# Second MLP products with shifted stationary operands (layer 0) and passes outermost (layer 1); third groups' scores in two column tiles

## The chip, the cores and the metric

The kernel runs on one core of a Trainium2 chip. The metric is the device time of one execution in microseconds (us). Before the change two executions were timed: 2586.64 and 2588.89 us, median 2587.76 us.

The core's engines are named as in the profile: PE is TensorE's matmul stream and PEld its loads of stationary operands, DVE is VectorE, ACT is ScalarE, POOL is GpSimd, and SP issues most of the DMAs.

## The reference

Two decoder layers on `x` of 1 x 1024 x 1024 in float32. Layer 0 mixes tokens with dilated sliding-window attention (8 heads, three groups of window and dilation (128, 1), (512, 4), (2048, 16)), layer 1 with gated linear attention; each is followed by an MLP with a squared ReLU.

```python
def dilated_attention(h, w_in, w_out):
    qkv = (h @ w_in).reshape(B, S, N_GROUPS, 3, ATTN_HEADS, HEAD_DIM)
    for g, (window, dil) in enumerate(DILATED_GROUPS):
        q = apply_rope(qkv[:, :, g, 0], cos, sin) * (HEAD_DIM ** -0.5)
        k = apply_rope(qkv[:, :, g, 1], cos, sin)
        o_g, lse_g = dilated_group_attention(q, k, qkv[:, :, g, 2], dil, window // dil)
    ...
def sq_relu_mlp(h, w_up, w_down):
    a = jax.nn.relu(h @ w_up)
    return (a * a) @ w_down

for i in range(DEPTH):
    h = rmsnorm(x, norm_mix_w[i])
    x = x + (dilated_attention(...) if i % 2 == 0 else gla_mixer(...))
    h = rmsnorm(x, norm_mlp_w[i])
    x = x + sq_relu_mlp(h, mlp_w_up[i], mlp_w_down[i])
return rmsnorm(x, final_norm_w)
```

The two products of an MLP are 1024 x 1024 by 1024 x 4096 and 1024 x 4096 by 4096 x 1024. The change touches the second one in both layers, and the scores q·k of the third attention group.

## The kernel before, in words

**Precision.** Large products are made in three passes. Each float32 operand is split into a rounded part (`h`, hi) and its remainder (`l`, lo), both of type fp32r; the sum is hi·hi + hi·lo + lo·hi, three matmuls into the same accumulator. ACT makes the hi part and DVE the lo part (`split`, lines 219 to 223). Scores and values of the attention are plain float32 matmuls, and the program runs each of those as two rows of the profile.

**Order.** All instructions are written out in the order in which each engine runs them (a manual schedule); semaphores carry only the dependences. PE's order in the attention comes from a clock of steps (`at`, `advance`), in which `Attention.plan` puts the four score blocks of a group at fixed steps, between matmuls of the next group's projection (`Heads.run_head`, which calls `Up.product`, line 599).

**The second MLP product** (`Down`). The product is computed in a scheme with 7 block products instead of 8 (`q` from 0 to 6, with the operand names in `ORDER`). Each has 8 steps `m`, so that there are 56 steps `n`. In step n:

- `product(n)` (line 1947) issues 24 matmuls 128x128 by 128x512: two contraction blocks `k`, four row blocks `t`, three passes. The stationary operand is a 128-column slice of the activations' parts (`sh`, `sl`), the moving one a row of the weights' parts (`th`, `tl`). Each row block `t` has a PSUM bank of its own: four banks `pA` or four banks `pB`, by the parity of q.
- `prep(n + 2)` makes the four parts of the step after next: `dh`, `dl` of the activations `sin`, `dh`, `dl` of the weights `t`.
- `fetch(n + 5)` and `load(n + 5)` issue the DMAs of `sin` and of the weights on SP.

Layer 0 has `spill` set (it writes its residual stream to DRAM), layer 1 has `spill` None.

**Memory.** SBUF tiles come from pools of equal slots. `k4` has 25 slots of 4096 bytes per partition, `h8` has 12 of 8192. A tile waits for the release of the slot that it gets. Every operand of the large matmuls lies in `k4` or `h8`, at a slice that begins at a multiple of 512 bytes, and the two pools' first slots differ by a multiple of 4096 bytes; so the start of a stationary slice and that of the moving slice differ by a multiple of 512 bytes. The exception is `wboth` (line 2418), a small gate weight of layer 1, whose eight stationary slices are 96 columns wide and 384 bytes apart.

**Scores of a group** (`Attention.scores`, line 989). For each head and group there are four calls `j` of two 128-row blocks. `keys_of` gives the keys of a block: one block of 128 keys for the third group (g = 2). There, each of the 8 heads has 8 products of 128x128 by 128x128.

Of the kernel before, what the change touches and what calls it, by code (L numbers as in the profile page):

```python
# [10 lines left out]
F32R = mybir.dt.float32r  # L11
# [9 lines left out]
P = 128  # L21
# [21 lines left out]
def hybrid_trunk(ctx, tc, x, norm_mix, norm_mlp, norm_fin, a_in, a_out, g_in, g_up, g_b, g_nw,  # L43
                 g_out, m_up, m_down, tab, msk, gmask, ident_d, out):
    nc = tc.nc
    pe, act, dve, pool, sp = nc.tensor, nc.scalar, nc.vector, nc.gpsimd, nc.sync

    cst = ctx.enter_context(tc.tile_pool(name="cst", bufs=1))
    wk = ctx.enter_context(tc.tile_pool(name="wk", bufs=1))
# [4 lines left out]
    def h8(shape, dt, name):  # L54
        return wk.tile(shape, dt, name=name, tag="h8", bufs=12)

    def k4(shape, dt, name):
        return wk.tile(shape, dt, name=name, tag="k4", bufs=25)

    def t2(shape, dt, name):  # L60
        return wk.tile(shape, dt, name=name, tag="t2", bufs=8)
# [7 lines left out]
    def bank(name):  # L69
        return psp.tile([P, 512], F32, name=name, tag="ps", bufs=8)  # L70
# [41 lines left out]
    class Weights:  # L112
# [17 lines left out]
        def dma(self):  # L130
            n = self.ndma
            if n < len(self.slots):
                self.ndma += 1
                src = self.slots[n]
                self.raws[n] = k4([P] + list(src.shape[1:]), F32, "raw")
                sp.dma_start(self.raws[n], src)

        def prep(self, eng=dve):
            n = self.nprep
            while self.ndma <= n:  # L140
                self.dma()
            src = self.raws.pop(n)
            self.nprep += 1
            if src.shape[-1] == RANK:
                both = self.both = k4([P, KT, 6 * RANK], F32R, "wboth")
                hi, lo = both[:, :, :RANK], both[:, :, RANK:2 * RANK]
            else:
                hi = k4(list(src.shape), F32R, "whi")
                lo = k4(list(src.shape), F32R, "wlo")
            by = self.by[n]  # L150
            if by is None:
                act.activation(hi, src, AF.Copy)
                eng.tensor_tensor(lo, src, hi.bitcast(F32), op=OP.subtract)
            else:
                act.activation(hi, src, AF.Copy, scale=by)
                eng.scalar_tensor_tensor(lo, src, by, hi.bitcast(F32), op0=OP.mult, op1=OP.subtract)
            if src.shape[-1] == RANK:
                for i in range(1, 3):
                    act.activation(both[:, :, 2 * RANK * i:2 * RANK * i + 2 * RANK], both[:, :, :2 * RANK], AF.Copy)
            self.parts[n] = (hi, lo)  # L160
# [57 lines left out]
    def split(hi, lo, src, on_act=True):  # L218
        if on_act:
            act.activation(hi, src, AF.Copy)  # L220
        else:
            dve.tensor_copy(hi, src)
        dve.tensor_tensor(lo, src, hi.bitcast(F32), op=OP.subtract)  # L223
# [277 lines left out]
    class Up:  # L501
# [82 lines left out]
        def product(self, p, s, ks=range(4)):  # L584
            w = self.part[p]
            if s == 6:
                wh, wl = w["d"][:, 0], w["d"][:, 1]
            else:
                wh, wl = (t[:, s % 2] for t in w["aabbgg"[s]])
            h = self.h[self.OPERANDS[s]]  # L590
            st = self.st.setdefault(p, {})
            b = "XYXVXZV"[s]
            first = s in (0, 1, 3, 5)
            if first and ks[0] == 0:
                st[b] = bank("p" + b)
            for k in ks:
                xh, xl = h.parts(k)
                for n, (u, v) in enumerate(((wh, xh), (wh, xl), (wl, xh))):
                    pe.matmul(st[b], u[:, k, :], v, start=first and k + n == 0, stop=k == 3 and n == 2,  # L599
                              skip_group_check=True)  # L600
# [351 lines left out]
    def keys_of(g, b):  # L952

        if g == 0:
            return (128 * (b - 1), 2, 0) if b else (0, 1, 128)
        if g == 1:
            return (256 * (b // 2), 2, 0) if b % 2 else (128 * b, 1, 128)
        return (128 * b, 1, 256)
# [20 lines left out]
    class Attention:  # L979
# [4 lines left out]
        def scores(self, j):  # L984
            ps = bank("pS").rearrange("p (i k) -> p i k", i=2)
            for i in range(2):
                b = 2 * j + i
                k0, n, m0 = keys_of(self.g, b)
                pe.matmul(ps[:, i, :128 * n], self.qT[:, 128 * b:128 * b + 128], self.kT[:, k0:k0 + 128 * n],
                          start=True, stop=True)  # L990
            self.st[j] = ps
# [771 lines left out]
    for p in range(heads.count):  # L1763
# [3 lines left out]
        if p == heads.count - 1:  # L1767
            for k in range(0, KT, 2):
                add_rows(a_out, k)
            c = 14 * p  # L1770
# [103 lines left out]
    class Down:  # L1874
# [32 lines left out]
        def prep(self, n):  # L1907
            if n >= 56:
                return
            q, m = divmod(n, 8)  # L1910
            kept = lambda x: x[m // 2][:, 2 * (m % 2):2 * (m % 2) + 2, :]
            sub = lambda o, a, b: dve.tensor_tensor(o, a, b, op=OP.subtract)  # L1912
            if q in (0, 4):
                t = self.raw.pop(n)
            elif q == 1:
                t = kept(self.br)
            elif q == 2:
                t = kept(self.tc)
                sub(t, t, kept(self.br))
            elif q == 3:  # L1920
                t = kept(self.tc)
                sub(t, self.raw.pop(n), t)
            elif q == 5:
                t = kept(self.br)
                sub(t, kept(self.tc), t)
            else:
                t = self.raw.pop(n)
                sub(t, t, kept(self.tc))
            got = []
            for src in (self.sin.pop(n), t):  # L1930
                hi, lo = k4([P, 2, 512], F32R, "dh"), k4([P, 2, 512], F32R, "dl")
                split(hi, lo, src)
                got += [hi, lo]
            self.cut[n] = got

        def product(self, n, blocks=range(4)):
            q, m = divmod(n, 8)
            s = "BABABAB"[q]
            fresh = q in (0, 1, 2, 6)
            if fresh and m == 0:  # L1940
                self.acc[s] = [bank("p" + s) for _ in range(4)]
            sh, sl, th, tl = self.cut[n]
            for k in range(2):
                for t in blocks:
                    c = slice(128 * t, 128 * t + 128)
                    for v, (a, b) in enumerate(((sh, th), (sh, tl), (sl, th))):
                        pe.matmul(self.acc[s][t], a[:, k, c], b[:, k, :], start=fresh and m + k + v == 0,  # L1947
                                  stop=m == 7 and k == 1 and v == 2, skip_group_check=True)

        def add(self, s, half, t, n):  # L1950
            tb = 4 * half + t
# [460 lines left out]
    for half in range(2):  # L2412
        ps = bank("pd")
# [70 lines left out]
```

## Time and profile before

| | |
|---|---|
| executions timed | 2586.64 and 2588.89 us, median 2587.76 |
| profiled execution, span from the first to the last instruction | 2586.6 us |
| PE busy | 2571.7 us (99%), 12000 matmul rows |
| PEld busy | 2142.3 us (83%) |
| DVE, ACT, POOL busy | 1862.7 (72%), 1298.2 (50%), 45.6 us (2%) |
| DMA | 443.73 MB, mean 172 GB/s |

The profiled execution's own time is not listed apart from its span; the two timed executions lie 0.0 and 2.3 us above that span. A line of the profile's fifth part or of its groups reads: line, engine, operation, out<-in by the program's names, shape, count, then the busy time of the group in us and the mean duration of one in ns. In a name `out<-in,in` the moving operand comes first, so `pB<-dl,dh` has the weights' remainder moving over the activations' rounded part. Matmuls overlap: each row lasts until its last result is out, while the next one has already begun. The rate is therefore read from the starts, or from the busy time of a group divided by its count, not from the mean duration.

The layers' second MLP products lie at 1257 to 1600 us (layer 0) and 2274 to 2587 us (layer 1); the attention's heads at about 265 to 880 us.

### The profile page before, as it was taken

The numbers are of one execution on the slowest core, as the hardware profiler recorded it, in microseconds if no ns is written. First come the engines' busy times: TensorE is split into PE (matmuls) and PEld (weight loads), VectorE is DVE, ScalarE is ACT, GpSimd is POOL, SyncE is SP. The second block draws the span as 40 slices with busy tenths as digits, with TensorE's granted clock in tenths as the row PEclk, the third lists the DMA queues.
The fourth block names the chain that finished last, engine by engine and source line by source line (L and its number), as shares of the span: only waits on it lengthen the run. The fifth ranks groups of instructions, "written<-read, shape, count | busy, mean of one in ns | idle before, by whom it ended". The sixth has DMA issues, their size and how long they took to land.

```text
span 2586.6 us, 33218 instructions
## 1 busy us (share of the span) xinstructions
PE 2571.7 (99%) x12000; PEld 2142.3 (83%) x12000; DVE 1862.7 (72%) x3018; ACT 1298.2 (50%) x2359; POOL 45.6 (2%) x71
## 2 busy tenths in 40 slices
PE   9999999999999999999999999999999999999998
PEld 7888888888888888888888888888888888888887
DVE  7745888888888768666566578887658766666567
ACT  7422455656665456555533345654326555553334
POOL 0000000000000000000000000000000000000000
PEclk9999999999999999999999999999999999999999
DMA  5543577778887634544865353463613544495544
GB/s 183 171 139 118 147 184 202 190 198 199 193 206 189 213 114 159 174 140 155 297 232 193 133 186 102 136 191 98 216 59 107 173 160 149 135 359 198 185 148 131
DMA packets 377544, 443.73 MB, mean 172 GB/s; under 512 B 64178, under 2 KB 240178, under 8 KB 377379
## 3 DMA queue, kind: packets, MB, share of 16 engines
q1 hardware_dynamic: 373650, 430.79, 54.1%
q0 software_dynamic: 3584, 10.56, 1.3%
q8 instruction: 94, 1.54, 0.2%
q14 instruction: 72, 0.58, 0.1%
q10 hardware_dynamic: 144, 0.26, 0.0%
HBM read 279.19 MB, written 126.62 MB: 157 GB/s over the span
## 4 chain that ended last, share of the span: by engine, by line
PE 64%; DVE 2%; ACT 1%; issue 0%; SPq 0%; DMA 0%; ACTq 0%; DVEq 0%
PE pB L1947 13%; PE pX L599 10%; PE pA L1947 10%; PE pV L599 7%; PE pY L599 3%; PE pZ L599 3%; PE pd L216 3%; PE pd L214 3%; PE pd L215 3%; PE pB L830 3%; PE pA L830 2%; PE pT L335 1%; PE pO L2245 1%; PE pU L2227 0%; PE pO L2244 0%; PE pT L260 0%
## 5 line engine op out<-in xcount | busy, mean ns | idle before, releaser
L1947 PE MATMUL pB<-dh 128*128 128x512 f32 x512 | 199.4, 389 | 0.0
L1947 PE MATMUL pB<-dh,dl 128*128 128x512 f32 x512 | 199.2, 389 | 0.0
L1947 PE MATMUL pB<-dl,dh 128*128 128x512 f32 x512 | 199.2, 389 | 0.0
L223 DVE TENSOR_TENSOR dl<-sin,dh 128x1024 fp32r<-128x1024 f32 x112 | 136.5, 1219 | 43.8 <-ACT dh L220 43.1
L220 ACT ACTIVATE dh<-sin 128x1024 fp32r<-128x1024 f32 x112 | 117.9, 1052 | 89.4 <-PE pB L1947 33.2
L220 ACT ACTIVATE dh<-kept 128x1024 fp32r<-128x1024 f32 x64 | 67.9, 1061 | 182.6 <-DVE kept L1912 137.8
L599 PE MATMUL pV<-s4h,wd 128*128 128x512 f32 x448 | 150.8, 398 | 0.0
L1947 PE MATMUL pA<-dh 128*128 128x512 f32 x384 | 149.4, 389 | 0.0
L1947 PE MATMUL pA<-dl,dh 128*128 128x512 f32 x384 | 149.4, 389 | 0.0
L1947 PE MATMUL pA<-dh,dl 128*128 128x512 f32 x384 | 149.4, 389 | 0.0
L1005 ACT ACTIVATE pt<-pt,orow 128x128 f32<-128x128 f32 (+1 forms) x192 | 84.5, 442 | 67.2 <-DVE orow L1003 65.4
L1947 PEld LDWEIGHTS pB<-dh,dl 128*128 128x128 f32 x512 | 96.1, 188 | 20.1
L1947 PEld LDWEIGHTS pB<-dl,dh 128*128 128x128 f32 x512 | 96.1, 188 | 19.8
L1947 PEld LDWEIGHTS pB<-dh 128*128 128x128 f32 x512 | 96.1, 188 | 19.8
L537 DVE TENSOR_TENSOR wal<-raw,wah 128x512 fp32r<-128x512 f32 x112 | 76.1, 685 | 41.4 <-ACT wah L536 41.4
L537 DVE TENSOR_TENSOR wbl<-t,wbh 128x1024 fp32r<-128x1024 f32 x56 | 68.6, 1225 | 44.0 <-ACT wbh L536 43.9
L608 ACT ACTIVATE c<-c 128x512 f32<-128x512 f32 x64 | 40.4, 631 | 118.5 <-DVE c L636 77.5
L599 PEld LDWEIGHTS pV<-s4h,wd 128*128 128x128 f32 x448 | 84.2, 188 | 17.7 <-DVE rb L624 0.2
L223 DVE TENSOR_TENSOR dl<-kept,dh 128x1024 fp32r<-128x1024 f32 x64 | 78.3, 1224 | 24.4 <-ACT dh L220 18.4
L599 PE MATMUL pZ<-a22h,wgh 128*128 128x512 f32 x224 | 89.9, 401 | 0.0
L604 ACT ACTIVATE e<-pX 128x512 f32<-128x512 f32 x96 | 56.5, 588 | 65.2 <-PE pX L599 65.0
L599 PE MATMUL pX<-s3h,wgh 128*128 128x512 f32 x224 | 88.6, 395 | 0.2 <-ACT e L1166 0.2
(398 smaller groups left out, 7397.5 us busy)
## 6 DMA issues: line engine op xcount, KB each, us to landing
sin<-acts SPq DMA_DIRECT2D x112, 512.0 KB, 3.8
raw<-in_mlp_w_up_dram SPq DMA_DIRECT2D x64, 512.0 KB, 5.7
acts<-s SPq DMA_DIRECT2D x64, 512.0 KB, 3.4
raw<-in_mlp_w_down_dram SPq DMA_DIRECT2D x64, 512.0 KB, 4.7
raw<-in_attn_w_in_dram SPq DMA_DIRECT2D x98, 256.0 KB, 4.9
cw<-c SPq DMA_DIRECT2D x192, 128.0 KB, 2.8
acts<-c SPq DMA_DIRECT2D x64, 256.0 KB, 2.2
kept<-in_mlp_w_down_dram SPq DMA_DIRECT2D x32, 512.0 KB, 4.7
```

What stands on the lines that cost most here:

```text
L214: pe.matmul(ps, sh, mh, start=start, stop=False)
L215: pe.matmul(ps, sh, ml, start=False, stop=False)
L216: pe.matmul(ps, sl, mh, start=False, stop=stop)
L220: act.activation(hi, src, AF.Copy)
L223: dve.tensor_tensor(lo, src, hi.bitcast(F32), op=OP.subtract)
L537: self.remain(lambda: dve.tensor_tensor(lo, src, hi.bitcast(F32), op=OP.subtract))
L599: pe.matmul(st[b], u[:, k, :], v, start=first and k + n == 0, stop=k == 3 and n == 2, skip_group_check=True)
L604: act.activation(e, self.st[p]["X"], AF.Copy)
L608: act.activation(r, r, AF.Relu)
L830: pe.matmul(self.acc[s][t], a[:, c], b[:, k, :], start=fresh and m + k + v == 0, stop=m == 1 and k == 1 and v == 2, skip_group_check=True)
L1005: act.activation(pt[:, i, :128 * n], pt[:, i, :128 * n], AF.Exp, scale=-1.0, bias=m, accum_out=self.row[:, r, HD:HD + 1])
L1947: pe.matmul(self.acc[s][t], a[:, k, c], b[:, k, :], start=fresh and m + k + v == 0, stop=m == 7 and k == 1 and v == 2, skip_group_check=True)
```

## The change

- Slots of `k4` become 1056 float32 wide (4224 bytes, 8 x 512 + 128) and there are 24 of them, not 25. A tile can begin at an offset `by` inside its slot.
- In layer 0's second MLP product the activations' parts (the stationary operands) begin at `4 * q + 4` float32 in their slots, 16 bytes for q = 0 up to 112 bytes for q = 6. The moving operands, and both operands of layer 1, begin at 0.
- In layer 1's second MLP product, for q = 0, 2 and 4, the three passes become the outer loop and the four row blocks the inner one. The other q keep their order.
- The third group's score products are issued as two matmuls of 64 stationary columns each, which write rows 0 to 63 and 64 to 127 of the same PSUM region.

What is computed is the same, with the same number of fp32r matmuls. All engines but PE keep the same instructions in the same order; the waits for `k4` slots differ, since tiles now fall into other slots.

```diff
-    def k4(shape, dt, name):
-        return wk.tile(shape, dt, name=name, tag="k4", bufs=25)
+    def k4(shape, dt, name, by=0):
+        t = wk.tile([P, 1056], dt, name=name, tag="k4", bufs=24)
+        n = math.prod(shape[1:])
+        t = t[:, by:by + n]
+        if len(shape) == 3:
+            return t.rearrange("p (a b) -> p a b", b=shape[2])
+        if len(shape) == 4:
+            return t.rearrange("p (a b c) -> p a b c", b=shape[2], c=shape[3])
+        return t
...
                 k0, n, m0 = keys_of(self.g, b)
+                if self.g == 2:
+                    for c in (0, 64):
+                        pe.matmul(ps[c:c + 64, i, :128], self.qT[:, 128 * b + c:128 * b + c + 64], self.kT[:, k0:k0 + 128],
+                                  start=True, stop=True)
+                    continue
                 pe.matmul(ps[:, i, :128 * n], self.qT[:, 128 * b:128 * b + 128], self.kT[:, k0:k0 + 128 * n],
...
             for src in (self.sin.pop(n), t):
-                hi, lo = k4([P, 2, 512], F32R, "dh"), k4([P, 2, 512], F32R, "dl")
+                by = 0 if src is t or self.spill is None else 4 * q + 4
+                hi, lo = k4([P, 2, 512], F32R, "dh", by), k4([P, 2, 512], F32R, "dl", by)
                 split(hi, lo, src)
...
             sh, sl, th, tl = self.cut[n]
+            both = ((sh, th), (sh, tl), (sl, th))
             for k in range(2):
-                for t in blocks:
+                order = [(t, v) for t in blocks for v in range(3)]
+                if self.spill is None and q in (0, 2, 4):
+                    order = [(t, v) for v in range(3) for t in blocks]
+                for t, v in order:
+                    a, b = both[v]
                     c = slice(128 * t, 128 * t + 128)
-                    for v, (a, b) in enumerate(((sh, th), (sh, tl), (sl, th))):
-                        pe.matmul(self.acc[s][t], a[:, k, c], b[:, k, :], start=fresh and m + k + v == 0,
-                                  stop=m == 7 and k == 1 and v == 2, skip_group_check=True)
+                    pe.matmul(self.acc[s][t], a[:, k, c], b[:, k, :], start=fresh and m + k + v == 0,
+                              stop=m == 7 and k == 1 and v == 2, skip_group_check=True)
```

Two places on PE show what moves. The first is in layer 0's attention, the first head's third group: the first two of its four calls, between matmuls of the next projection (`pX`, `pV`). Before:

```order
L599 MATMUL pX_2540<-s2h_617,wbl_2481 128x512
L989 MATMUL pS_2662<-kT_2558,qT_2437 128x128 x2
L989 MATMUL pS_2665<-kT_2558,qT_2437 128x128 x2
L599 MATMUL pV_2623<-s4h_695,wd_2562 128x512
L599 MATMUL pV_2623<-s4l_696,wd_2562 128x512
```

and after:

```order
L606 MATMUL pX_2540<-s2h_617,wbl_2481 128x512
L998 MATMUL pS_2662<-kT_2558,qT_2437 64x128 x4
L998 MATMUL pS_2667<-kT_2558,qT_2437 64x128 x4
L606 MATMUL pV_2623<-s4h_695,wd_2562 128x512
L606 MATMUL pV_2623<-s4l_696,wd_2562 128x512
```

Nothing else moves there: four products of 128 rows have become eight of 64 rows, at the same place in PE's order. The second place is one contraction block of the first product (q = 0) of layer 1's second MLP product; the number of a `pB` is its row block's PSUM bank. Before:

```order
L1947 MATMUL pB_19205<-dh_19133,dh_19129 128x512
L1947 MATMUL pB_19205<-dl_19134,dh_19129 128x512
L1947 MATMUL pB_19205<-dh_19133,dl_19130 128x512
L1947 MATMUL pB_19206<-dh_19133,dh_19129 128x512
L1947 MATMUL pB_19206<-dl_19134,dh_19129 128x512
L1947 MATMUL pB_19206<-dh_19133,dl_19130 128x512
```

and after:

```order
L1964 MATMUL pB_19269<-dh_19197,dh_19193 128x512
L1964 MATMUL pB_19270<-dh_19197,dh_19193 128x512
L1964 MATMUL pB_19271<-dh_19197,dh_19193 128x512
L1964 MATMUL pB_19272<-dh_19197,dh_19193 128x512
L1964 MATMUL pB_19269<-dl_19198,dh_19193 128x512
L1964 MATMUL pB_19270<-dl_19198,dh_19193 128x512
```

Before, three matmuls in a row went to one bank and the stationary part changed after two of them; after, four in a row have the same moving operand, each goes to another bank, and the stationary slice changes at each.

## The prediction

> **What bounds the kernel now.** I read the page first, then PE's waits, then the rate of PE in the stages that the change touches. From the page, the busy times, the granted clock and the head of the chain that ended last:
>
> ```profile
> span 2586.6 us, 33218 instructions
> PE 2571.7 (99%) x12000; PEld 2142.3 (83%) x12000; DVE 1862.7 (72%) x3018; ACT 1298.2 (50%) x2359; POOL 45.6 (2%) x71
> ...
> PEclk9999999999999999999999999999999999999999
> ...
> PE 64%; DVE 2%; ACT 1%; issue 0%; SPq 0%; DMA 0%; ACTq 0%; DVEq 0%
> ```
>
> PE is busy in 2571.7 of 2586.6 us, and the clock is granted in full throughout (a 9 is 90% or more). PE's own waits, longest first:
>
> ```profile
> PE pS L989 <- DVE qT L1146: 1.6, 4, 0.6
> PE warm L1373 <- POOL warm L1348: 1.3, 1, 1.3
> PE pO L1069 <- ACT pt L1018: 0.9, 1, 0.9
> PE pB L830 <- DVE dl L815: 0.8, 1, 0.8
> ```
>
> The longest sum is 1.6 us, so no wait is worth removing and the time is PE's: the number of matmuls times what each takes. A busy PE is not PE at its peak, so the rate per matmul matters. For line 1947, the second MLP product, over the whole span and over 280 us of layer 1 in which nothing else runs on PE (columns: stretch, its length, PE busy with count, PEld busy with count):
>
> ```profile
> 0.00:2587.00 2587.00, 610.16 (x2688) 504.43 (x2688) 1.00 0.56 172
> 2280.00:2560.00 280.00, 280.00 (x1237) 231.86 (x1236) 1.00 0.61 206
> ```
>
> 610.16 us / 2688 is 227.0 ns for each; in the undisturbed stretch 1236 intervals fill 280 us, 226.5 ns. The starts show that it is the same in every pass (layer 0):
>
> ```profile
> 1399.66 0.39 PE L1947 MATMUL pA<-dl,dh 128*128 128x512 f32 x1
> 1399.89 0.39 PE L1947 MATMUL pA<-dh,dl 128*128 128x512 f32 x1
> 1400.12 0.39 PE L1947 MATMUL pA<-dh 128*128 128x512 f32 x1
> 1400.34 0.39 PE L1947 MATMUL pA<-dl,dh 128*128 128x512 f32 x1
> ```
>
> The first interval keeps the stationary operand's part and changes the moving one's, the second and the third change the stationary slice, the third also the PSUM bank between row blocks; all are 0.22 to 0.23 us.
>
> **The change part by part.**
>
> *Passes outermost, layer 1.* The same 24 matmuls and 24 loads of a step come in another order; there are 3 x 8 x 24 = 576 of them. Every kind of neighbour that the new order has (same moving operand with another bank, a change of the stationary slice at each) occurs in the rows above at the same interval, and each matmul has its own load already (x2688 against x2688), so none is saved. Cost 0. The lo part of the moving operand is needed three matmuls later at a step's start, which PE did not wait for anyway.
>
> *Distances, layer 0.* 7 x 8 x 24 = 1344 matmuls get stationary slices 16 to 112 bytes away from the old alignment. Can alignment matter? The one fp32r product whose stationary slices do not lie at multiples of 512 bytes from the moving ones is `wboth`, 96 columns wide and 384 bytes apart. Its row and the first row of the next half frame eight matmuls:
>
> ```profile
> 1722.55 0.39 PE L2418 MATMUL pd<-a11h,wboth 128*96 128x512 f32 x1
> ...
> 1723.25 0.39 PE L2418 MATMUL pd<-a11l,wboth 128*96 128x512 f32 x1
> 1723.48 0.40 PE L2418 MATMUL pd<-a11h,wboth 128*96 128x512 f32 x1
> ...
> 1724.40 0.39 PE L2418 MATMUL pd<-a12h,wboth 128*96 128x512 f32 x1
> ```
>
> 1.85 us / 8 is 231 ns, 4.5 above the 226.5 of the other products although less is loaded. So the interval is not a constant of the form; whether the distance or the width does it, these rows cannot tell. The lower bound is the fastest 512-wide interval in the trace, that of the bfloat16 warming matmuls:
>
> ```profile
> 7.40 0.38 PE L1373 MATMUL warm<-warm 128*128 128x512 bf16 x1
> 7.40 1.46 PE L1373 MATMUL warm<-warm 128*128 128x512 bf16 x6
> ```
>
> (1.46 - 0.38) / 5 = 0.216 us, 11 ns less than 227. The term lies between 1344 x -11 ns = -14.8 us and 1344 x +4.5 ns = +6.0 us. I take 0, by the 2688 rows of the same form, which no slot pair changes. The Trainium skill, "TensorE: Matmul & The Clock Gate", Part 2, says that TensorE reads its moving operand and its loads through two independent ports, so that loading the next operand takes nothing from the running matmul; by that the term is 0 at any distance, and the `wboth` rows are what the trace has against it.
>
> *Slots of 4224 bytes.* 4224 is 8 x 512 + 128, so all operands in `k4`, in every large product, now differ by multiples of 128 bytes and no longer of 512. I take 0 for this by the same row; it is the third rival.
>
> *One slot of `k4` fewer.* Loads are already held back by slots; from SP's waits, the two largest at line 1888, and from the tile `sin`, the time its DMAs take:
>
> ```profile
> SPq L1888 <- PE pB L1947: 144.3, 31, 9.9
> SPq L1888 <- PE pA L1947: 134.8, 30, 7.0
> DMA to landing us min/median/max: 3.4/3.8/13.8
> ```
>
> On SP all later loads and stores are queued behind such a wait. A step is 24 x 0.227 = 5.4 us and takes about six `k4` tiles, so a slot comes on average 0.9 us later and at worst one step. A load is issued five steps ahead and used by `prep` three steps later, 16.3 us; less the 3.8 us to land that leaves 12.5, more than 5.4. The preparation runs two steps (10.9 us) ahead; its pieces:
>
> ```profile
> L220 ACT ACTIVATE dh<-sin x112: 1040/1047/1081, 1247.5 to 2556.5; 128x1024 fp32r<-128x1024 f32 x112
> L223 DVE TENSOR_TENSOR dl<-sin,dh x112: 1210/1218/1228, 1248.6 to 2559.4; 128x1024 fp32r<-128x1024 f32 x112
> L1912 DVE TENSOR_TENSOR kept<-kept x32: 1211/1217/1220, 1318.7 to 2513.3; 128x1024 f32<-128x1024 f32 x32
> ```
>
> Done one after the other without overlap, two of the first, two of the second and one of the third are 5.7 us, against the 5.4 that a delay of a whole step would leave: 0.3 us late where the worst comes together, and cover everywhere else. Between 0 and, with such a miss at every seventh of the 107 steps, 15 x 0.3 = 4.6 us; I take 2. A gain is excluded, since fewer slots release nothing earlier.
>
> *Scores in two column tiles.* 8 heads x 8 products are 64, run as two rows each: 128 of the 208 rows of this group are the third group's. The timeline at the first head's third group:
>
> ```profile
> L989 PE MATMUL pS<-kT,qT 128*128 128x128 f32 x208 | 32.6, 275 | 1.7 <-DVE qT L1146 1.2 <-DVE c L1129 0.6
> ...
> 328.46 0.39 PE L599 MATMUL pX<-s2h,wbl 128*128 128x512 f32 x1
> 328.69 1.05 PE L989 MATMUL pS<-kT,qT 128*128 128x128 f32 x8
> 329.49 0.48 PE L599 MATMUL pV<-s4h,wd 128*128 128x512 f32 x1
> 329.81 0.40 PE L599 MATMUL pV<-s4l,wd 128*128 128x512 f32 x1
> ```
>
> From 328.69 to 329.81 there are eight score rows and one 512-wide matmul: (1.12 - 0.227) / 8 = 0.112 us for a row; the change of form costs nothing beside it. All 128 rows are 14.3 us of PE. After the change they are 256 rows with half the stationary columns but the same 128 moving ones.
> Side by side, two halves take what one whole took, and only the last row of a sequence stands alone. There are 18 sequences (two per head, and four for the last head, whose calls stand apart): 18 x 0.112 = +2.0 us. One after the other: 128 more rows, +14.3 us. Below: if a half row cost a quarter of a whole one, 256 x 0.028 = 7.2, a gain of 7.2 us, for which no row speaks.
> To this comes what PE pays on entering and leaving the divided form, 36 times. No row shows it. If PE must finish the running matmul first, it is that matmul's tail, 0.389 (the mean of a 512-wide row) less 0.227 = 0.162 us, 5.8 us in all; at the other end 0, as at the change from 512-wide to score rows above. If the next load also cannot run ahead, 0.19 us more each time (59.2 us for 384 loads overlap; one lasts 190 ns), 6.8 us:
>
> ```profile
> L989 PEld LDWEIGHTS pS<-kT,qT 128*128 128x128 f32 x384 | 59.2, 190 | 10.9 <-DVE qT L1146 2.5 <-DVE c L1129 1.0 <-PE pO L1069 0.7
> ```
>
> I take side by side with the tail, 2.0 + 5.8 = +7.8 us; the ends are -7.2 and 14.3 + 5.8 + 6.8 = +26.9 us. The Trainium skill, "TensorEngine Tiling (Array Packing)", Key Properties, says that tiles load and multiply in parallel and that a change of the tiling mode drains TensorE; the trace has no divided matmul to confirm either. Without a drain the sum would be 5.8 us less.
>
> *Sum.* 2586.6 + 0 + 0 + 2 + 7.8 = 2596.4 us against the profiled span. The median of the timed runs lies 1.2 us above that span, which gives 2597.6, or 2597.
>
> **The rivals.**
>
> 1. *The halves run one after the other*, in the 18 places of layer 0's attention. For it: PE's matmuls begin in order, and the rows of one product are strictly spaced by 0.112 us. Against it: nothing in the trace. +14.3 + 5.8 + 2 gives 2587.8 + 22 = 2610 us, 2617 with loads that cannot run ahead. This is the slower end; it decides as soon as a half row takes more than half of 0.112 us.
> 2. *The distances free layer 0's matmuls.* At 216 ns in all seven passes -14.8 us, 2583; at some of them in between. If the slot pitch alone did this for line 1947 and for the 1094.57 us of line 599 too, (2688 + 4704) x -11 ns = -81 us, 2516.
>
> ```profile
> 0.00:2587.00 2587.00, 1094.57 (x4704) 877.78 (x4704) 1.00 0.56 172
> ```
>
> 3. *The new pitch spoils the regular interval.* If operands at 128-byte multiples run as the `wboth` rows do, three slot pairs of four are hit: 7392 x 3/4 x 4.5 ns = +25 us, 2623; more if the bad intervals are the rule. It would pass +2% (42 us more than the forecast) from 7.6 ns for each of those 5544 matmuls.
> 4. *The lost slot starves PE* at every step, 0.3 us x 107 = 32 us in place of 2, 2628. The 12.5 us of slack of the loads speaks against it.
> 5. *Nothing shows*: no drain, side by side, no distance effect. +2 to +4 us; it lies beside the forecast and shares its chance.
>
> **How the numbers follow.** Forecast with the fifth case 0.46, first rival 0.22, second 0.14, third 0.14, fourth 0.04. The likeliest gives 2597 us. The range reaches down to 2575 (all seven distances free and the scores at no cost, 2587.8 - 14.8 + 2) and up to 2624 (the first rival's 2617 and the third's 2623); left out are what is worse in the third and fourth and a pitch that frees the whole kernel. One measurement of this kernel can tell about 2%, 52 us, from no change: below 2536 only the second rival in its widest form comes (0.02), above 2639 the third at its worst or the fourth with the first (0.04), within 2% the rest (0.94).
>
> **What would show it.** Right: line 1964's group at 227 ns for a matmul in both layers and in all q; 256 score rows at line 998 whose starts interleave, with the next `pV` about 1.2 us after the first row of a sequence; PE's sums of waits still of a few us. Wrong: intervals that differ between the stretches of the seven q, or in line 606; 16 score rows that take 1.8 us; SP's wait at line 1900 turning into PE waits for `dh` or `dl`.

## The result, and the profile after

The kernel after the change takes 2630.88 us (2630.61 and 2631.15 us), before it 2587.76 us: ratio 1.0167, 95% interval 1.0137 to 1.0196, 43.1 us more. The prediction said 2597 us with a range up to 2624 us; the time lies above that range. From the page of the changed kernel, span and PE's busy time:

```profile
span 2629.4 us, 33543 instructions
...
PE 2616.3 (100%) x12128; PEld 2143.3 (82%) x12128; DVE 1867.2 (71%) x3018; ACT 1299.4 (49%) x2359; POOL 45.6 (2%) x71
```

PE was busy in 2571.7 us and is now in 2616.3 us, 44.6 more; the whole loss is longer PE work. The longest of PE's waits:

```profile
PE warm L1385 <- POOL warm L1360: 1.3, 1, 1.3
...
```

No wait is longer than before (the longest sum was 1.6 us), so the missing slot does not make PE wait. Which matmuls became longer is seen in the busy time by line. First line 606 (the product that was line 599), then line 1964 (the second MLP product, line 1947 in the kernel before), over the whole span; then line 1964 in layer 0 and in layer 1:

```profile
0.00:2630.00 2630.00, 1112.40 (x4704) 879.25 (x4704) 1.00 0.54 169
0.00:2630.00 2630.00, 623.84 (x2688) 504.92 (x2688) 1.00 0.54 169
...
1277.94:1593.80 315.86, 312.85 (x1344) 252.25 (x1343) 1.00 0.58 198
2311.34:2622.40 311.06, 310.99 (x1344) 252.29 (x1343) 1.00 0.56 194
```

Line 1964 rose from 610.16 to 623.84 us, 232.1 ns for each in place of 227.0. It did so in both layers: 232.8 ns in layer 0, where operands are shifted, but 231.4 ns also in layer 1, where none is. Line 606, which the change doesn't name at all, rose from 1094.57 to 1112.40 us. What these have in common is the pool `k4`. The starts in layer 0 (q = 3), the first and the last of eleven rows:

```profile
1421.77 0.39 PE L1964 MATMUL pA<-dl,dh 128*128 128x512 f32 x1
...
1424.08 0.40 PE L1964 MATMUL pA<-dh,dl 128*128 128x512 f32 x1
```

The ten intervals between the eleven starts take 2.31 us, 231 ns each; in the rows of before in the prediction they were 0.22 or 0.23 us. The third groups' scores, at the same place as in the prediction:

```profile
332.84 0.39 PE L606 MATMUL pX<-s2h,wbl 128*128 128x512 f32 x1
333.16 1.09 PE L998 MATMUL pS<-kT,qT 128*64 128x128 f32 x16
334.19 0.50 PE L606 MATMUL pV<-s4h,wd 128*128 128x512 f32 x1
334.52 0.39 PE L606 MATMUL pV<-s4l,wd 128*128 128x512 f32 x1
```

From the last matmul ahead of the scores to the second one behind them it is 1.68 us; before it was 329.81 - 328.46 = 1.35 us. A sequence of four products costs 0.33 us more. The trace has 17 sequences (the prediction counted 18, but two of the last head's calls stand together), so 5.6 us is the estimate for all.

### The profile page after: what moved, and what is told of

It is laid out like the page before. It is cut to its first block, busy times and chain, and to the rows that moved or that the text cites. A ratio compares the mean times of both kernels' runs of the same rounds, so it can differ in the third digit from the quotient of the medians.

```text
span 2629.4 us, 33543 instructions
## 1 busy us (share of the span) xinstructions
PE 2616.3 (100%) x12128; PEld 2143.3 (82%) x12128; DVE 1867.2 (71%) x3018; ACT 1299.4 (49%) x2359; POOL 45.6 (2%) x71
## 4 chain that ended last, share of the span: by engine, by line
PE 97%; DVE 1%; DMA 1%; ACT 1%; issue 0%; SPq 0%; ACTq 0%; DVEq 0%
PE pX L606 17%; PE pB L1964 13%; PE pV L606 12%; PE pA L1964 10%; PE pB L837 8%; PE pA L837 6%; PE pZ L606 6%; PE pY L606 6%; PE pd L221 3%; PE pd L223 3%; PE pd L222 3%; PE pO L1081 2%; PE pS L1001 2%; PE pT L342 1%; PE pB L1481 1%; PE pS L998 1%
## 5 line engine op out<-in xcount | busy, mean ns | idle before, releaser
L1964 PE MATMUL pB<-dh 128*128 128x512 f32 x512 | 178.6, 394 | 0.0
L1964 PE MATMUL pB<-dl,dh 128*128 128x512 f32 x512 | 178.2, 394 | 0.0
L1964 PE MATMUL pB<-dh,dl 128*128 128x512 f32 x512 | 178.1, 393 | 0.0
L606 PE MATMUL pX<-s2h,wbh 128*128 128x512 f32 x224 | 89.0, 397 | 0.0
```

## The experiments

The theory to be tested: the pitch of 4,224 B (the distance from one slot to the next) is the cause, because operand starts now differ by changing multiples of 128 B in every fp32r product that uses `k4`. Rivals: the seven distances of layer 0, the missing slot, the order of the passes.

**One part alone: the pitch.** The kernel before with the 24 new slots, and nothing else.

```diff
-        return wk.tile(shape, dt, name=name, tag="k4", bufs=25)
+        t = wk.tile([P, 1056], dt, name=name, tag="k4", bufs=24)
+        n = math.prod(shape[1:])
+        t = t[:, :n]
...
```

> The kernel before with one thing of the change: the 24 slots of 4,224 B instead of 25 of 4,096 B (every tile still begins at its slot's first byte; layer-0 distances, pass order and whole scores as before). Theory (the pitch makes operand starts differ by changing multiples of 128 B in every fp32r product that takes an operand from these slots, so that the interval no longer holds at 226.7 ns): +37 to +41 us, ratio 1.014 to 1.016, with intervals of 231 to 232 ns in both layers, and no row of waits over 2 us. Rival (the seven distances of layer 0 are what costs): within +-5 us. Rival (the lost slot costs): +37 to +41 us as well, but with new waits of PE in the list of waits and intervals of 226.7 ns between them.

Measured: 2623.58 us against 2587.24 us, ratio 1.0141 (1.0126 to 1.0156), +36.3 us, a little under the 37 to 41 us expected. The page, and the busy time of lines 606 and 1954 (first and second MLP products here):

```profile
span 2621.3 us, 33269 instructions
...
PE 2609.2 (100%) x12000; PEld 2145.5 (82%) x12000; DVE 1866.0 (71%) x3018; ACT 1298.5 (50%) x2359; POOL 45.6 (2%) x71
```

```profile
0.00:2630.00 2630.00, 1112.15 (x4704) 879.38 (x4704) 1.00 0.54 169
0.00:2630.00 2630.00, 622.49 (x2688) 505.10 (x2688) 1.00 0.54 169
```

Five sixths of the loss come with the new slots. The two lines rose by 17.6 and 12.3 us, 3.7 and 4.6 ns for each matmul. PE's busy time rose by 37.5 us in all, while the rest of the span, 14.9 us before, shrank to 12.1: together the 34.7 us between the two spans.

**All but the pitch and the distances.** The kernel after with 24 slots of 4,096 B and all tiles at their slots' first bytes: the missing slot, the passes outermost and the half scores stay.

```diff
-        t = wk.tile([P, 1056], dt, name=name, tag="k4", bufs=24)
+        t = wk.tile([P, 1024], dt, name=name, tag="k4", bufs=24)
...
-                by = 0 if src is t or self.spill is None else 4 * q + 4
+                by = 0
```

> The kernel after with slots of 4,096 B (24 of them) and without the distances of layer 0: what remains is the slot that is missing, the passes outermost in layer 1 and the scores in halves. Theory (pitch): +4 us over before (2 to 7), the scores in halves alone (27.3 us in the after trace against 23.4 before), intervals back at 226 to 227 ns. Rival (lost slot or passes outermost cost): +35 us or more, as after. Rival (layer-0 distances): +4 to +20 us.

Measured: 2592.11 against 2587.24 us, ratio 1.0019 (1.0010 to 1.0029), +4.9 us. Line 1964:

```profile
0.00:2630.00 2630.00, 610.16 (x2688) 504.52 (x2688) 1.00 0.54 169
```

Line 1964 takes 610.16 us, to the last digit what it took before, although 576 of its matmuls come with the passes outermost. So the pass order costs nothing and frees nothing. The +4.9 us lie within the 2 to 7 us expected.

**The disputed cost by itself.** A probe issues 72 matmuls per series, in the order of a step, and varies only where the operands begin (`SH`, `SL`, `TH`, `TL` are multiples of 512 B; `hi`, `lo`, `tl` the shifts in float32):

```diff
+        both = ((SH + hi, TH), (SH + hi, TL + tl), (SL + lo, TH))
+        for r in range(reps):
+            for k in range(2):
+                order = [(t, v) for t in range(4) for v in range(3)]
...
+                for t, v in order:
+                    a, b = both[v]
+                    mm(ps, a + 512 * k + step * t, b + 512 * k, n)
```

> A probe, not the kernel: it leaves out the whole reference computation (its output is a copy of x and one PSUM bank) and issues only the matmuls in question, so only the profile's intervals count. Each series is 72 matmuls (128 stationary columns by 512 moving columns, fp32r) in the order of a step of the second MLP product: first part by first part, first part by remainder, second part by first part. The series differ in where the stationary parts and the moving remainder begin past a multiple of 512 B from the moving first part. The interval of a series is its busy time less 162 ns, over 72. Theory (operand starts): one constant distance in a series may be regular whatever it is, near 226.7 ns as in the second MLP products of before; series with distances that change from matmul to matmul (names with two or three y) stand 4 to 6 ns higher, as in the trace after (229.6 to 232.4 ns). Rival (a distance is good or bad by itself): series of one distance already differ by 4 ns or more. Rival (nothing in TensorE depends on operand starts): all series within 1 ns of each other. The same probe has passes outermost (theory and prediction: no difference), narrower stationary operands, and float32 128x128 products whole and as two 64-column halves: 2 to 16 products, halves cheaper by some 109 ns against 0.2 us per whole product, with an entry and exit of some 0.1 to 0.5 us for each sequence.

The groups by tile, in the view's order of busy time. `dNNNNx` has both stationary parts NNNN bytes from the moving ones, `m000y128y000x` the second part alone at 128 B, `outer0x` the passes outermost, `w96x` 96 columns at multiples of 512 B and `w96by384x` at multiples of 384 B:

```profile
L35 PE MATMUL d0096x<-big 128*128 128x512 f32 x72 | 17.0, 396 | 0.0
...
L35 PE MATMUL d0128x<-big 128*128 128x512 f32 x72 | 17.0, 395 | 0.0
...
L35 PE MATMUL d0384x<-big 128*128 128x512 f32 x72 | 17.0, 395 | 0.0
...
L35 PE MATMUL w96by384x<-big 128*96 128x512 f32 x72 | 16.9, 394 | 0.0
...
L35 PE MATMUL m000y128y000x<-big 128*128 128x512 f32 x72 | 16.8, 394 | 0.0
...
L35 PE MATMUL w96x<-big 128*96 128x512 f32 x72 | 16.7, 392 | 0.0
...
L35 PE MATMUL d0192x<-big 128*128 128x512 f32 x72 | 16.6, 391 | 0.0
...
L35 PE MATMUL outer0x<-big 128*128 128x512 f32 x72 | 16.5, 389 | 0.0
...
L35 PE MATMUL d0016x<-big 128*128 128x512 f32 x72 | 16.5, 389 | 0.0
L35 PE MATMUL d0256x<-big 128*128 128x512 f32 x72 | 16.5, 389 | 0.0
L35 PE MATMUL d0000x<-big 128*128 128x512 f32 x72 | 16.5, 389 | 0.0
```

A group's busy time is 71 intervals and the last row's own duration. The same for `d0000x` and `d0128x`, in this order, from the windows, which have two decimals:

```profile
0.00:1446.50 1446.50, 16.48 (x72) 13.51 (x72) 1.00 0.02 7
...
0.00:1446.50 1446.50, 16.96 (x72) 13.51 (x72) 1.00 0.02 7
```

(16.48 - 0.389) / 71 = 226.6 ns at 0 B, (16.96 - 0.395) / 71 = 233.3 ns at 128 B. My expectation that one constant distance would be regular whatever it is fell: series of one constant distance already differ. In this probe 0, 16 and 256 B are good, 96, 128 and 384 B cost 6.7 ns or a little more, 192 B stands between. The values come again after 256 B, not after 512. No series is below that at 0 B, so the regular interval of before is the best that a distance gives. A mixture (0 and 128 B) stands at (16.8 - 0.394) / 71 = 231 ns, as the kernel after does. A mixture does not cost what its parts cost: in this one a third of the matmuls is at 128 B, which alone would be 2.2 ns each, and it loses 4.4; with the first stationary part shifted by 128 B in place of the second (`m128y000y000x`, two thirds at 128 B), it is the full 233.3 ns.

**The period, in the kernel.** If only the distance modulo 256 B counts, a pitch of 4,352 B (17 x 256) is harmless, and layer 0's distances can be had without the pitch's loss. There are 23 such slots, 100,096 B in place of 102,400. Two runs: the kernel before with them, and the kernel after with them. The edit is shown against the kernel after; in the kernel before the same line takes the place of the 25 slots of 4,096 B, as in `pitch_alone`:

```diff
-        t = wk.tile([P, 1056], dt, name=name, tag="k4", bufs=24)
+        t = wk.tile([P, 1088], dt, name=name, tag="k4", bufs=23)
```

> The kernel before with 23 slots of 4,352 B (17 times 256 B) instead of 25 of 4,096 B, nothing else. In the probe the interval came back at every 256 B: 226.7 ns at 0, 16, 240, 256, 272, 512 B, and 233.3 ns at 128 B and 384 B. Theory (only the distance modulo 256 B counts): two slots fewer and a pitch that is no multiple of 512 B cost nothing in the intervals, 226.7 ns in both layers, and the time is that of before, within +-3 us (unless the second lost slot makes PE wait, which would show as rows of waits). Rival (any pitch off 512 B upsets the interval): +30 us or more, as with 4,224 B.

Measured: 2598.27 against 2587.85 us, ratio 1.0041 (1.0026 to 1.0055), +10.4 us, outside the 3 us of the expectation. The second MLP product (line 1954), and PE's waits:

```profile
0.00:2630.00 2630.00, 610.16 (x2688) 504.36 (x2688) 1.00 0.55 169
```

```profile
PE pA L837 <- DVE c L852: 2.7, 1, 2.7
...
PE pA L837 <- DVE dl L822: 1.9, 2, 0.9
...
```

The interval is the old one to the last digit, so a pitch off 512 B is harmless by itself. What is lost is the exception of the expectation: with two slots fewer PE waits for operands in line 837 (products of the token mixers of both layers, line 830 before; the wait of 2.7 us lies in layer 1), and the span outside PE's busy time grows from 14.9 to 20.7 us (2596.1 less 2575.4 us). The rest, 3.7 us, is busy time, 3.5 of it in line 837 itself (350.11 to 353.63 us). There the granted clock explains most of it: within the 2.7 us wait began 6.83 us in which it was 0.50, and matmuls in it start 0.43 us apart and not 0.23 (some 12 of them, 2.4 us more). What brought the clock down is not shown: in `pitch_aligned` it was 0.50 from 841.39 to 844.80 us with PE busy throughout. Line 837 of `pitch_4352` in its stretch, the granted clock behind the two counts:

```profile
1683.44:1690.27 6.83, 4.98 (x12) 3.92 (x13) 0.50 0.31 115
```

> The kernel after with 23 slots of 4,352 B instead of 24 of 4,224 B; its seven distances in layer 0 (16 to 112 B), its passes outermost and its half scores stay. Theory (distance modulo 256 B): the first q of layer 0 (16 B) holds 226.7 ns, the six others stand at 232.0 to 234.3 ns as the probe's series of 32 to 112 B, which is 192 x (6.6 + 6.7 + 6.7 + 5.3 + 7.6 + 6.6) ns = +7.6 us; layer 1 is back at 226.7 ns; with +4.9 us of rest_alone +12.5 us over before (10 to 15). Rival (distances matter only where they change from matmul to matmul): +4 to +6 us, as rest_alone. Rival (any pitch off 512 B): +40 us.

Measured: 2609.05 against 2587.85 us, ratio 1.0087 (1.0072 to 1.0102), +21.2 us. Line 1964 in the stretches of q = 0, 1, 4 and 5 of layer 0, and in all but the end of layer 1:

```profile
1261.66:1305.18 43.52, 43.52 (x192) 36.04 (x192) 1.00 0.93 338
1305.18:1349.97 44.79, 44.79 (x193) 36.06 (x192) 1.00 0.66 235
...
1439.57:1484.11 44.54, 44.54 (x194) 36.04 (x193) 1.00 0.41 142
1484.11:1529.09 44.98, 44.98 (x194) 36.16 (x192) 1.00 0.47 164
...
2295.56:2599.97 304.41, 304.41 (x1343) 252.06 (x1343) 1.00 0.57 198
```

Each stretch holds the starts of 192 matmuls: 226.7 ns at 16 B (q = 0), 233.3 at 32 B, 232.0 at 80 B, 234.3 at 96 B, and 226.7 again in layer 1 (304.41 us / 1343). These are the values on which the expectation's 7.6 us stood; the distances cost by themselves. The total is above the 12.5 us expected, which held no price for the second missing slot; with its 10.4 us the sum is 22.9, near the 21.2 measured.

**The pitch kept, its effect taken away.** The same 24 slots of 4,224 B at the same addresses; tiles whose slot begins at a multiple of 256 B start 128 B into it (the others begin 128 B past such a multiple; line 612, which reads `k4` and `h8` together, shows below that the two pools fit). `EVEN` has one bit for each tile, in the order in which they are made. The edit against `pitch_alone`:

```diff
-        t = t[:, :n]
...
+        by = 32 * (EVEN >> made[0] & 1)
+        made[0] += 1
+        t = t[:, by:by + n]
```

> The same 24 slots of 4,224 B as in pitch_alone, at the same addresses, but every tile that falls into a slot that begins at an even multiple of 128 B starts 128 B into it, so that all tiles start at the same place modulo 256 B. Theory (only the distance of the operand starts modulo 256 B counts): the +36 us of pitch_alone are gone, intervals 226.7 ns in both layers, time within +-3 us of before. Rival (pitch, slot size or the missing slot cost): +30 us or more, as pitch_alone.

Measured: 2587.08 against 2587.52 us, ratio 0.9998 (0.9989 to 1.0008). Lines 612 and 1960, the first and second MLP products:

```profile
0.00:2630.00 2630.00, 1094.62 (x4704) 877.82 (x4704) 1.00 0.54 169
0.00:2630.00 2630.00, 610.16 (x2688) 504.52 (x2688) 1.00 0.54 169
```

The 36 us are gone, with the slots' size, number and addresses unchanged. This settles the cause in this kernel: neither the pitch as such nor the 25th slot, but where operands start against each other modulo 256 B.

**The halves alone.** The kernel before with the half scores only.

```diff
+                if self.g == 2:
+                    for c in (0, 64):
+                        pe.matmul(ps[c:c + 64, i, :128], self.qT[:, 128 * b + c:128 * b + c + 64], self.kT[:, k0:k0 + 128],
+                                  start=True, stop=True)
+                    continue
```

> The kernel before with the third groups' scores as two column halves and nothing else (25 slots of 4,096 B, no distances, passes inside). Theory: all that is left over in rest_alone comes from the halves: +4 to +6 us, since the probe shows a pair of halves 6 to 7 ns apart every 109 ns against 111.6 ns for a whole pass (next to no gain), and 318 against 228 ns of entry and some 0.2 us more at the exit of each sequence. Rival (lost slot or passes outermost carry a part of it): +0 to +3 us.

Measured: 2591.64 against 2587.52 us, ratio 1.0016 (1.0007 to 1.0025), +4.1 us (1.8 to 6.5). So the halves can account for all of `rest_alone`'s 4.9 us, which lie in this interval.

**What of a matmul feels the distance.** A second probe alternates two products; some series have shorter moving parts or other types. `stAAAmvBBBx` has both stationary parts at AAA bytes and both moving parts at BBB bytes past a multiple of 512; in `own000nextNNNx` each product's own two operands are 0 B apart and the next product's stationary part is NNN bytes from the moving part in use (by turns ahead of it and behind it), and in `ownNNNnext000x` it is the other way round.

```diff
+                a = SH + st[i] + 512 * (r % 3) + 128 * (2 * (r % 2) + i)
+                b = TH + mv[i] + 512 * (r % 3)
+                pe.matmul(ps[:, :n], src[:, a:a + 128], src[:, b:b + n], start=True, stop=True, skip_group_check=True)
```

> A second probe; it leaves out the whole reference computation again (output: a copy of x and one PSUM bank). Two products alternate, 72 in each series. Names: st and mv are the starts of the stationary and the moving part in bytes past a multiple of 512 B. Theory 1 (distance, not place): st128mv128, st064mv064 and st096mv096 stay at 226.7 ns; st000mv128 rises to 233.3 ns. Theory 2 (the load of the next stationary part reads while the moving part before it is read, so the distance between those two counts): own000next128 rises to about 233 ns, own128next000 stays near 226.7 ns. Rival to 2 (the distance between a product's own two operands counts): the reverse. Shorter moving parts (n128, n256, n384), bfloat16 and float32 operands: theory 2 expects some nanoseconds per product wherever a load lies wholly beside moving reads; if the loss grows with the columns read beside the load, n256 loses about half of n512. Rival: fp32r with 512 columns is the only form that loses.

The groups by tile, in the view's order; `bf` is bfloat16, `fp` float32, `n256` has 256 moving columns, and the number is the distance in bytes:

```profile
L62 PE MATMUL fp000x<-raw 128*128 128x512 f32 x48 | 20.8, 592 | 0.0
...
L62 PE MATMUL fp128x<-raw 128*128 128x512 f32 x48 | 20.8, 592 | 0.0
...
L62 PE MATMUL own000next096x<-big 128*128 128x512 f32 x72 | 17.0, 396 | 0.0
L62 PE MATMUL st016mv000x<-big 128*128 128x512 f32 x72 | 17.0, 396 | 0.0
L62 PE MATMUL st000mv128x<-big 128*128 128x512 f32 x72 | 17.0, 395 | 0.0
...
L62 PE MATMUL own128next000x<-big 128*128 128x512 f32 x72 | 16.7, 392 | 0.0
L62 PE MATMUL own000next128x<-big 128*128 128x512 f32 x72 | 16.6, 391 | 0.0
L62 PE MATMUL st128mv128x<-big 128*128 128x512 f32 x72 | 16.5, 390 | 0.0
L62 PE MATMUL bf000x<-bfb 128*128 128x512 bf16 x72 | 15.7, 379 | 0.0
...
L62 PE MATMUL bf128x<-bfb 128*128 128x512 bf16 x72 | 15.7, 379 | 0.0
...
L62 PE MATMUL n256by000x<-big 128*128 128x256 f32 x72 | 8.8, 283 | 0.0
...
L62 PE MATMUL n256by064x<-big 128*128 128x256 f32 x72 | 8.6, 281 | 0.0
```

Both operands shifted alike by 128 B: no loss (16.5 us); only the moving one shifted: the full loss (17.0). So the place alone costs nothing, the distance does. But the distance is not all: `st016mv000x`, 16 B apart, takes (16.96 - 0.396) / 71 = 233.3 ns here, where `d0016x` of the first probe took 226.8. The two series have the same distances modulo 512 B and differ in which operands follow each other, so whether 16 B costs hangs on more than the distance. bfloat16 and float32 take the same at 0 and at 128 B; among these types only fp32r loses. With 256 moving columns the order turns round: (8.8 - 0.283) / 71 = 120 ns at 0 B, (8.6 - 0.281) / 71 = 117 ns at 64 B. The `own`/`next` series were to tell whether a product's own two operands or the next load and the running product get in each other's way. At 128 B they rise to 230 and 229 ns, neither to 233 nor to 226.7. At 96 B `own000next096x` reaches 234.4 ns, as theory 2 of the expectation has it, but `own096next000x` stands at 230.1 and not at 226.7. So neither theory 2 nor its rival is borne out. Why a distance costs stays open.

## Why the prediction was wrong, point by point

- **What bounds the kernel: right.** PE was the bound and stayed it, and no wait of PE grew to matter.
- **Passes outermost, 0: right.** `rest_alone` has 610.16 us in line 1964, as before; `outer0x` is as fast as `d0000x`.
- **Distances in layer 0, 0 with bounds -14.8 to +6.0 us: wrong.** On a good pitch they cost 617.67 - 610.16 = 7.5 us (line 1964 of `after_4352`, row below), beyond the upper bound, which came from `wboth`. Those rows mixed two things, width and distance: in the probe 96 columns cost already without the odd distance (16.7 against 16.5 us, 3.4 ns for each matmul), and more with it (16.9). The lower bound, the bfloat16 interval, was not reached by any distance tried.

```profile
0.00:2630.00 2630.00, 617.67 (x2688) 504.86 (x2688) 1.00 0.54 169
```

  In the kernel after, the same distances add little, since the pitch has spoiled the intervals already: 312.85 us in layer 0 against 311.44 us in `pitch_alone`, +1.4 us. Layer 0 of `pitch_alone`, line 1954:

```profile
1271.16:1585.61 314.45, 311.44 (x1344) 252.27 (x1343) 1.00 0.57 198
```

- **Slots of 4224 bytes, 0: the step that failed.** It took the term as 0 "by the same row", the regular interval of operands whose starts always differ by multiples of 512 B. That row could say nothing of other distances, and the one row that had another distance was slower. Measured: +36.3 us (`pitch_alone`), and nothing once all starts agree modulo 256 B (`pitch_aligned`): the fp32r interval rose where the sum kept it as it was.
- **Third rival, +25 us: the right mechanism at too small a price.** It counted 5544 matmuls, three quarters of two lines, at 4.5 ns. The loss of 3.7 to 4.6 ns is the mean over all 7392 of them, 29.9 us. With a period of 256 B a pitch of 4,224 B gives only the distances 0 and 128 B, so half of the pairs and not three quarters would be hit; but mixtures lose more than the share of their bad pairs, as the first probe has it. The mixers' line 837 (350.11 to 355.57 us, +5.5) and the helper of the output projections (lines 221 to 223, +2.8 together), which draw on `k4` too, weren't counted. A chance of 0.14 looks low for it: the only row with an odd distance spoke for it.
- **One slot fewer, +2 us: cover was complete.** `pitch_aligned` has 24 slots at 0.9998 (0.9989 to 1.0008). With one more gone there is a cost (`pitch_4352`, +10.4 us), so the cover was nearly used up.
- **Scores in halves, +7.8 us: right mechanism, size off.** +4.1 us (1.8 to 6.5). The profile has 0.33 us for a sequence of four products, where the step had 0.112 + 2 x 0.162 = 0.436; and there are 17 sequences, not 18. The first rival (one after the other) is out: 16 half rows from 333.16 to 334.19 take 1.03 us together with the exit, not 1.8. The Trainium skill, "TensorEngine Tiling (Array Packing)", Key Properties, says that tiles work in parallel and that a change of the mode drains TensorE. The first agrees with these 1.03 us. A pause on entering is there, 0.32 us from the start of the last matmul ahead to the first half row in place of 0.23; but that row starts at 333.16, before the recorded end of the matmul ahead (332.84 + 0.39 = 333.23), so these rows don't show that PE was empty.
- **The Trainium skill's rule on the two read ports** ("TensorE: Matmul & The Clock Gate", Part 2: loading the next operand takes nothing from the running matmul) would have it that no distance matters. The bfloat16 series agree (15.7 us at 0 and at 128 B); the fp32r series show a loss (16.48 and 16.96 us), and the second probe could not tell whether the loading causes it.
- **Sum.** +36.3 (pitch) + 4.9 (rest) + 1.4 (distances on top) = 42.6 us against the 43.1 measured.

## What to carry to other kernels

When PE is the bound, an interval that is the same in every row can be a property of how the operands lie, and a change of a pool's pitch can take it from all products that use the pool, the untouched ones too. Before padding a slot, work out the operand starts against each other: here a distance of 0 modulo 256 B was free for fp32r with 512 columns in all the series shown (within 0.7 ns of 226.6), 16 B was free in one probe and in the kernel with 4,352 B (q = 0) and cost 3% in the other probe, and most others cost 1 to 3%. A term for which the trace of before has only one kind of row should get a chance and a price from the one odd row, not zero from the many regular ones.

## What the runs showed of the hardware that was not expected

- The fp32r interval with 512 moving columns depends on where the stationary operand begins against the moving one: in the first probe with a period of 256 B, 226.6 ns at 0 B and 233.3 ns at 128 B, with the clock granted in full. The distance alone does not give it (16 B: 226.8 ns in one probe, 233.3 in the other).
- A pair of 64-column halves saves nothing in float32, even in a long sequence. From the timeline of the first probe, whole products (16 of them) and halves, each with the group that follows:

```profile
1424.53 3.73 PE L73 MATMUL whole16x<-raw 128*128 128x128 f32 x32
1428.01 5.70 PE L35 MATMUL aftwhole16x<-big 128*128 128x512 f32 x24
1433.64 3.71 PE L79 MATMUL halves16x<-raw 128*64 128x128 f32 x64
1437.29 3.01 PE L35 MATMUL afthalves16x<-big 128*128 128x512 f32 x12
```

  From the first row to the next group it is 3.48 us for whole products and 3.65 us for halves: twice as many rows take 0.17 us more than the whole ones, entering and leaving included.
